# The sum of two weight blocks by an accumulating DMA, half-size weight tiles and alternating steps in a two-branch encoder block

## The chip, the cores and the metric

One core of one Trainium2 chip runs the kernel. The metric is the device time of one execution in microseconds; the median of three runs is compared.

## What is computed

The reference is one residual block of a streaming encoder on 256 tokens of width 4096, all in float32. Cut to what matters:

```python
h = rms_norm(x, pre_norm_gain)
proj = h @ w_in                      # 4096 x 24704, split into q, k, v, gate_a, qi, ki, wi,
                                     # z, xs, bm, cm, dt_raw, merge_logits (2 x 4096)
y_a = dsa_attention(q, k, v, qi, ki, wi) * silu(gate_a)      # [256, 2048]
y_b = ssd_mixer(xs, z, bm, cm, dt_raw, ...)                  # [256, 2048]
gates = sigmoid(merge_logits).reshape(b, s, 2, 4096)
merged = gates[0] * (y_a @ w_branch_attn) + gates[1] * (y_b @ w_branch_ssd)
out = merged @ w_out                                         # 4096 x 4096
x = x + rms_norm(out, post_norm_gain)
```

## The kernel before

Every matmul of the projections is computed as three: activation and weight are each split into a high part (float32r) and a low part, and `low x high + high x low + high x high` is accumulated in PSUM. The high part of a weight chunk (`wh`) is a ScalarE copy, the low part (`wl`) a VectorE subtraction. A matmul has 128 tokens as its stationary and 512 weight columns as its moving side.

*Plain stages.* `gemm` (L138) computes 512 output columns for both token tiles from eight chunks of 1 MB (`raw`, 128 x 4 x 512, pool `rawp` with three buffers, L54), loaded by SP. A chunk is split in two halves of 128x1024 (L168, L169). The index projection, the attention projections, the SSD projections and the first gate columns run so, up to about 1611 us, and the last two column blocks of the output projection at the end. In the first `gemm`, `prep_x` (L223) also loads the transposed input `xr` and issues the weight load itself; for chunk 0 it issues slices of both in turn. `make_rstd` (L244) loads the input rows once more in eight pieces `xn` for the row norms.

*Pair stages.* `pair_gemm` (L738) takes 512 columns of two blocks at a time, and two 128-row tiles of the contraction a step, so the weight chunk of a step is a 2x2 block matrix b11, b12, b21, b22 (`_quads`, L1072, lays the blocks out as b12, b11, b22, b21), and the activations of the two token tiles are a 2x2 block matrix too. A step of kind "S" multiplies them with seven products: the weights are b11, b21, b22 and four sums t1 = b11 - b12, t3 = b22 - b12, t2 = b22 + t1, t4 = b21 - t2; the activations are four blocks and four sums S1 to S4 that `make_ext` (L692) has formed. A step of kind "D" or "R" takes eight products. Sums over steps stay in PSUM, in banks 1 to 8, and `early` (L758) and `late` (L766) put the output blocks together from them: `early` after the last S step, `late` at the end of the group. `SX`, `SY` and `SM` (L34 to L36) say which of the 16 steps are S, for the gates, the branch projections and the output projection; `plain` ranges make some of them R.

The pair stages are: seven gate groups of 16 steps (`GATES`), eight branch groups of eight steps, three output groups of 16 steps. There are 90 S steps (21 matmuls each) and 134 others (24 each).

In an S step VectorE forms t1 and t3 in one operation `t13` (L792), and t2 (L795) and t4 (L797) in place in `raw`; four calls of `split` (L728; L731 on ScalarE, L732 on VectorE) make the high and low parts, in tiles of the pools `whp` and `wlp`, four buffers each. A step of eight products has two calls of `split`.

*Order.* Waits come from the tile framework. It lays out each engine's instructions when the kernel is built, and each engine runs its own in that order. Small work (rotary, attention, scan, epilogues, forms) is written as generators, and `step()` runs one piece of them after each half chunk or step. POOL's queue holds the stores of the gates to DRAM (`sscr`, L852), of the merged rows (`mscr`, L926) and the loads of activations for the forms (`fr`, L866 and L871). SP's queue holds the weight loads (L154, L786) and the loads of gates (L907).

## Time and profile before

| | |
|---|---|
| median of three runs | 2912.79 us (2911.95 to 2913.32) |
| the profiled execution | 2915.75 us, of it 2914.0 us of span from the first to the last instruction |
| TensorE, matmul rows | 2875.6 us busy, 99% |
| TensorE, weight-load rows | 2356.7 us, 81% |
| VectorE | 2039.2 us, 70% |
| ScalarE | 1499.5 us, 51% |
| GpSimd | 210.4 us, 7% |
| granted TensorE clock | 0.998 of full speed |
| DMA | 592 MB, 203 GB/s on average |

A busy share counts the time in which at least one row of the engine is open. Matmul rows overlap, since one begins while the one before still drains; so TensorE's share says little of its pace, and the distance between the starts of two matmuls says more.

### The profile page before, as it was taken

Reading aid. Unit: us, or ns where it says so; the run is one execution under the profiler, and the core shown is the slowest. Engines: PE = TensorE matmul, PEld = TensorE weight load, DVE = VectorE, ACT = ScalarE, POOL = GpSimd, SP = SyncE. Lnnn points to the kernel's source line nnn. Section 1 sums busy time; section 2 is a strip of 40 time slices with the busy share of each in tenths; the row PEclk is TensorE's granted clock in tenths of the full one; section 3 lists DMA queues with packets and bytes.
Section 4 is the critical chain, followed back from the end, with each engine's and each line's share of the span. In section 5 each row is a group of like instructions: output and inputs, shape, how many; then the busy total and the mean of one; then the engine's idle time right before and its main releaser. Section 6 shows DMA issues by size and latency. Waiting matters only on the chain. (4 is left out here: it accounts for less than half of the span.)

```text
span 2914.0 us, 33808 instructions
## 1 busy us (share of the span) xinstructions
PE 2875.6 (99%) x12990; PEld 2356.7 (81%) x12990; DVE 2039.2 (70%) x2490; ACT 1499.5 (51%) x1799; POOL 210.4 (7%) x209
## 2 busy tenths in 40 slices
PE   9999999999999999999999999999999999999997
PEld 7878888888888888888888888878887777788786
DVE  6677445454554646565657998989887888888975
ACT  7444443444434445454555555555565544555554
POOL 0100001000010012121211000000000000000001
PEclk9999999999999999999999999999999999999999
DMA  9545555555555555555555565555566556655664
GB/s 343 187 159 176 188 185 183 194 177 194 175 195 188 181 177 179 186 181 178 177 191 193 202 224 217 217 218 213 222 239 229 223 216 224 254 220 197 221 248 159
DMA packets 96098, 592.25 MB, mean 203 GB/s; under 512 B 11328, under 2 KB 12096, under 8 KB 30528
## 3 DMA queue, kind: packets, MB, share of 16 engines
q1 hardware_dynamic: 88992, 567.02, 54.2%
q0 software_dynamic: 6944, 23.07, 2.2%
q8 instruction: 102, 1.67, 0.2%
q14 instruction: 60, 0.49, 0.0%
HBM read 570.12 MB, written 19.92 MB: 202 GB/s over the span
## 5 line engine op out<-in xcount | busy, mean ns | idle before, releaser
L169 DVE TENSOR_TENSOR wl<-raw,wh 128x1024 fp32r<-128x1024 f32 x563 | 699.0, 1243 | 597.5 <-ACT wh L168 595.3
L168 ACT ACTIVATE wh<-raw 128x1024 fp32r<-128x1024 f32 x563 | 596.5, 1060 | 795.6 <-PE p L179 754.6
L177 PE MATMUL p<-wh,b 128*128 128x512 f32 x2304 | 911.1, 396 | 1.4 <-ACT wh L165 1.4
L178 PE MATMUL p<-wl,b 128*128 128x512 f32 x2304 | 898.7, 390 | 3.5 <-DVE wl L169 3.3
L179 PE MATMUL p<-wh,b 128*128 128x512 f32 x2304 | 898.4, 390 | 0.0
L756 PE MATMUL p<-wh,b 128*128 128x512 f32 x2300 | 757.2, 391 | 4.5 <-ACT wh L731 3.2
L731 ACT ACTIVATE wh<-raw 128x1024 fp32r<-128x1024 f32 (+1 forms) x538 | 510.5, 984 | 312.9 <-PE p L756 214.4
L732 DVE TENSOR_TENSOR wl<-raw,wh 128x1024 fp32r<-128x1024 f32 (+1 forms) x538 | 584.3, 1130 | 82.5 <-ACT wh L731 79.5
L756 PEld LDWEIGHTS p<-wh,b 128*128 128x128 f32 x2300 | 430.6, 188 | 101.3 <-ACT wh L731 11.2
L178 PEld LDWEIGHTS p<-wl,b 128*128 128x128 f32 x2304 | 433.3, 188 | 93.2 <-DVE wl L169 4.4
L177 PEld LDWEIGHTS p<-wh,b 128*128 128x128 f32 x2304 | 432.8, 188 | 92.3 <-ACT wh L165 3.0
L179 PEld LDWEIGHTS p<-wh,b 128*128 128x128 f32 x2304 | 432.6, 188 | 91.5
L756 PE MATMUL p<-wl,b 128*128 128x512 f32 x1150 | 448.5, 390 | 2.2 <-DVE wl L732 2.1
L756 PE MATMUL p<-wh,ext 128*128 128x512 f32 x1104 | 387.1, 391 | 4.8 <-ACT wh L731 4.8
L756 PEld LDWEIGHTS p<-wl,b 128*128 128x128 f32 x1150 | 215.9, 188 | 49.3 <-DVE wl L732 4.5
L756 PEld LDWEIGHTS p<-wh,ext 128*128 128x128 f32 x1104 | 207.2, 188 | 52.3 <-ACT wh L731 10.7
L756 PE MATMUL p<-wl,ext 128*128 128x512 f32 x552 | 217.2, 394 | 4.4 <-DVE wl L732 4.4
L731 ACT ACTIVATE wh<-t 128x1024 fp32r<-128x1024 f32 x90 | 95.5, 1061 | 146.0 <-PE p L756 120.8
L756 PEld LDWEIGHTS p<-wl,ext 128*128 128x128 f32 x552 | 103.6, 188 | 33.1 <-DVE wl L732 12.0
L792 DVE TENSOR_TENSOR t<-raw 128x1024 f32<-128x1024 f32 x90 | 109.9, 1221 | 28.7 <-DMA raw<-w_gate_d 14.7
L732 DVE TENSOR_TENSOR wl<-t,wh 128x1024 fp32r<-128x1024 f32 x90 | 109.9, 1222 | 16.5 <-ACT wh L731 15.7
L283 POOL TENSOR_TENSOR ro<-m,m 128x512 f32<-128x512 f32 (+1 forms) x26 | 43.0, 1666 | 413.9 <-DVE m L281 407.3
(224 smaller groups left out, 1415.1 us busy)
## 6 DMA issues: line engine op xcount, KB each, us to landing
raw<-w_attn_d SPq DMA_DIRECT2D x128, 1024.0 KB, 4.7
raw<-w_gate_d SPq DMA_DIRECT2D x128, 1024.0 KB, 4.8
raw<-w_ssd_d SPq DMA_DIRECT2D x96, 1024.0 KB, 4.7
raw<-w_br_d SPq DMA_DIRECT2D x64, 1024.0 KB, 4.8
raw<-w_out_d SPq DMA_DIRECT2D x64, 1024.0 KB, 4.8
raw<-w_qi_d SPq DMA_DIRECT2D x31, 1024.0 KB, 6.6
sg<-sscr SPq DMA_DIRECT2D x32, 256.0 KB, 3.4
sscr<-pc POOLq DMA_DIRECT2D x28, 256.0 KB, 2.9
```

Source lines behind the costliest of these rows:

```text
L168: A.activation(wh, rs, AF.Copy)
L169: V.tensor_sub(wl, rs, wh.bitcast(F32))
L177: T.matmul(ps[t], al[:, tk], wh[:, i, :], start=first, stop=False)
L178: T.matmul(ps[t], ah[:, tk], wl[:, i, :], start=False, stop=False)
L179: T.matmul(ps[t], ah[:, tk], wh[:, i, :], start=False, stop=last)
L283: G.tensor_add(ro, m1, m2)
L731: A.activation(h, src, AF.Copy)
L732: V.tensor_sub(l, src, fbit(h))
L756: T.matmul(ps[j], l, r, start=first and n == 0, stop=left[j] == 0 and n == 2)
L792: V.tensor_sub(t13, raw[:, 1:3, :], raw[:, 0:1, :].to_broadcast([P, 2, NW]))
```

## The change

It has five parts. (1) In an S step, b12's tile row gets the sum b12 + b11 by a DMA that POOL issues and that adds to what SP's load put there; the signs of b12 and b22's use are turned so that every combination is built on this sum. In eight-product steps the parts of b12 and b22 are split with a factor of -1, and the epilogue subtracts where it added. The four-row operation `t13` is gone; three one-row sums are left. (2) A weight chunk is two tiles of 512 KB, eight buffers of them, loaded one after the other. (3) The S steps of the gates and the output projection are the odd ones; those of the branches are 1, 4, 7, 9, 12, 15. (4) Products come in another order, and in a group's last S step products 1, 6, 7 come first, with `early` behind them. (5) To make room, `tab` and `mb` move to the attention pool, `xn` becomes sixteen pieces in the `yr` tiles, and the x slices of chunk 0 are all issued ahead of its weights.

```diff
+RBUFS = 8
...
-SX = (1, 3, 5, 6, 8, 10, 12, 14)
-SY = (1, 4, 6, 9, 12, 14)
-SM = (1, 3, 5, 6, 8, 10, 12, 14)
+SX = tuple(range(1, 16, 2))
+SY = (1, 4, 7, 9, 12, 15)
+SM = SX
...
-    rawp = root(tc.tile_pool(name="rawp", bufs=3))
+    rawp = root(tc.tile_pool(name="rawp", bufs=RBUFS))
...
+    def raw_tile():
+        return rawp.tile([P, HK, NW], F32, tag="raw", name="raw")
+
+    def load_half(raw, chunk, hf, each=False):
+        if each:
+            for i in range(HK):
+                nc.sync.dma_start(raw[:, i, :], chunk[:, hf * HK + i, :])
+        else:
+            nc.sync.dma_start(raw, chunk[:, hf * HK:(hf + 1) * HK, :])
...
-            raw = raws.get(c)
-            if raw is None:
-                raw = raws[c] = rawp.tile([P, KC, NW], F32, tag="raw", name="raw")
+            if half not in raws:
+                raws[half] = raw_tile()
                 if prep is not None:
-                    xr = prep(c, raw, chunks[c])
+                    if not hf:
+                        xr = prep_x(c)
+                    load_half(raws[half], chunks[c], hf, c == 0)
                 else:
-                    nc.sync.dma_start(raw, chunks[c])
+                    load_half(raws[half], chunks[c], hf)
             if half not in parts:
                 wh = whp.tile([P, HK, NW], F32R, tag="wh", name="wh")
                 wl = wlp.tile([P, HK, NW], F32R, tag="wl", name="wl")
                 parts[half] = wh, wl
                 if len(parts) > WBUFS:
                     del parts[next(iter(parts))]
-                rs = raw[:, hf * HK:(hf + 1) * HK, :]
+                rs = raws[half]
...
-    def prep_x(c, raw, chunk):
+    def prep_x(c):
         xr = sp.tile([P, KC, S], F32, tag="xr", name="xr")
         if c == 0:
             for i in range(KC):
                 nc.sync.dma_start(xr[:, i, :], xT[c][:, i * S:(i + 1) * S])
-                nc.sync.dma_start(raw[:, i, :], chunk[:, i, :])
         else:
             nc.sync.dma_start(xr.rearrange("p k t -> p (k t)"), xT[c])
-            nc.sync.dma_start(raw, chunk)
...
-            for h in range(4):
-                xn = sp.tile([P, D // 4], F32, tag="xn", name="xn")
-                nc.sync.dma_start(xn, x[t * P:(t + 1) * P, h * (D // 4):(h + 1) * (D // 4)])
+            for h in range(8):
+                xn = yr.tile([P, NW], F32, tag=f"yr{h}", name="xn")
+                nc.sync.dma_start(xn, x[t * P:(t + 1) * P, h * NW:(h + 1) * NW])
                 A.activation(xn, xn, AF.Square, accum_out=ss[:, t, h:h + 1])
-                yield
                 yield
...
-            V.scalar_tensor_tensor(f[:, 0, :], a21, -1.0, a22, ALU.mult, ALU.subtract)
+            V.tensor_sub(f[:, 0, :], a22, a21)
             V.tensor_sub(f[:, 2, :], a11, a21)
             V.scalar_tensor_tensor(f[:, 1, :], f[:, 0, :], -1.0, a11, ALU.mult, ALU.subtract)
-            V.tensor_sub(f[:, 3, :], a12, f[:, 1, :])
+            V.scalar_tensor_tensor(f[:, 3, :], a12, -1.0, f[:, 1, :], ALU.mult, ALU.subtract)
...
-    def split(src, n):
+    def split(src, n, sign=1):
         h = whp.tile([P, n, NW], F32R, tag="wh", name="wh")
         l = wlp.tile([P, n, NW], F32R, tag="wl", name="wl")
-        A.activation(h, src, AF.Copy)
-        V.tensor_sub(l, src, fbit(h))
+        A.activation(h, src, AF.Copy, scale=float(sign))
+        if sign < 0:
+            V.scalar_tensor_tensor(l, src, -1.0, fbit(h), ALU.mult, ALU.subtract)
+        else:
+            V.tensor_sub(l, src, fbit(h))
...
-                for o, j in zip(d, (2, 5, 4)):
-                    A.activation(o, ps[j], AF.Copy)
-                V.tensor_add(d[3], ps[8], d[1])
-                V.tensor_add(d[1], ps[3], d[1])
+                for o, j, sc in zip(d, (2, 5, 4), (1.0, -1.0, 1.0)):
+                    A.activation(o, ps[j], AF.Copy, scale=sc)
+                V.tensor_sub(d[3], d[1], ps[8])
+                V.tensor_sub(d[1], d[1], ps[3])
                 return
             c11, c12, c21, c22 = dest
             V.tensor_add(c12, ps[5], c12)
-            V.tensor_add(c22, ps[5], c21)
+            V.scalar_tensor_tensor(c22, ps[5], -1.0, c21, ALU.mult, ALU.subtract)
             V.tensor_add(c11, ps[2], c11)
             V.tensor_add(c21, ps[4], c21)
-            V.tensor_add(c12, ps[3], c12)
+            V.scalar_tensor_tensor(c12, ps[3], -1.0, c12, ALU.mult, ALU.subtract)
             if 8 in ps:
-                V.tensor_add(c22, ps[8], c22)
+                V.tensor_sub(c22, c22, ps[8])
...
+            ra, rb = raw_tile(), raw_tile()
+            load_half(ra, chunk(i), 0)
+            if kind == "S":
+                nc.gpsimd.dma_start(ra[:, 0, :], chunk(i)[:, 2, :], accum_op=ALU.add)
+            load_half(rb, chunk(i), 1)
             if n in hooks:
                 hooks[n]()
             assert kind_of[i] == what, (n, i, kind_of, len(aux))
             if kind == "S":
-                t13 = tp.tile([P, 2, NW], F32, tag="t13", name="t13")
-                V.tensor_sub(t13, raw[:, 1:3, :], raw[:, 0:1, :].to_broadcast([P, 2, NW]))
-                b11, b22 = split(raw[:, 1:3, :], 2)
-                b21, = split(raw[:, 3:4, :], 1)
-                V.tensor_add(raw[:, 2, :], raw[:, 2, :], t13[:, 0, :])
-                t1, t3 = split(t13, 2)
-                V.tensor_sub(raw[:, 3, :], raw[:, 3, :], raw[:, 2, :])
-                t2, t4 = split(raw[:, 2:4, :], 2)
-                for j, name, w in ((1, "A11", b11), (2, "A12", b21), (3, "S4", b22),
-                                   (5, "S1", t1), (7, "S3", t3), (6, "S2", t2), (4, "A22", t4)):
-                    product(j, i, name, w)
-                early()
+                b11, b21 = split(rb, 2)
+                t1, b22 = split(ra, 2)
+                V.tensor_add(ra[:, 1, :], ra[:, 0, :], ra[:, 1, :])
+                V.tensor_sub(rb[:, 0, :], ra[:, 1, :], rb[:, 0, :])
+                V.tensor_add(rb[:, 1, :], ra[:, 1, :], rb[:, 1, :])
+                t2, = split(ra[:, 1:2, :], 1)
+                t3, t4 = split(rb, 2)
+                now = {1: ("A11", b11), 2: ("A12", b21), 3: ("S4", b22), 4: ("A22", t4),
+                       5: ("S1", t1), 6: ("S2", t2), 7: ("S3", t3)}
+                for j in (1, 6, 7, 5, 3, 2, 4) if n == len(plan) - 1 else (1, 2, 5, 3, 6, 7, 4):
+                    product(j, i, *now[j])
+                    if j == 7:
+                        early()
             else:
                 w = {}
-                for k in (1, 2):
-                    w[k, 2], w[k, 1] = split(raw[:, 2 * k - 2:2 * k, :], 2)
-                todo = [(k, j) for k in (1, 2) for j in
-                        ((5, 2, 4, 3) if kind == "D" else (2, 4, 3, 8))]
-                if n == len(plan) - 1:
-                    todo.sort(key=lambda kj: (5, 2, 4, 3, 8).index(kj[1]))
+                w[1, 2], w[2, 2] = split(ra, 2, -1)
+                w[1, 1], w[2, 1] = split(rb, 2)
+                todo = [(k, j) for j in ((5, 3, 2, 4) if kind == "D" else (3, 8, 2, 4))
+                        for k in (1, 2)]
...
-            order = (0, 2, 4, 7, 1, 9, 3, 11, 5, 13, 6, 15, 8, 12, 10, 14)
-            plain = (8, 12, 10, 14)
+            order = (0, 2, 4, 6, 1, 8, 3, 10, 5, 12, 7, 14, 9, 11, 13, 15)
+            plain = (9, 11, 13, 15)
...
-    b = [v[:, 0][..., c2], v[:, 0][..., c1], v[:, 1][..., c2], v[:, 1][..., c1]]
+    b = [v[:, 0][..., c2], v[:, 1][..., c2], v[:, 0][..., c1], v[:, 1][..., c1]]
...
```

## Rows read from the trace of the kernel before

**Rows 1.** The page, busy time of an engine (share of the span) and its instructions.

```profile
PE 2875.6 (99%) x12990; PEld 2356.7 (81%) x12990; DVE 2039.2 (70%) x2490; ACT 1499.5 (51%) x1799; POOL 210.4 (7%) x209
```

**Rows 2.** Timeline of TensorE in a gate group: start us, us, what.

```profile
1814.20 0.39 PE L756 MATMUL p<-wh,b 128*128 128x512 f32 x1
...
1817.84 0.39 PE L756 MATMUL p<-wh,ext 128*128 128x512 f32 x1
```

**Rows 3.** Stretch, its us; busy us (count) of PE, PEld, DVE, ACT, POOL; clock, DMA, GB/s.

```profile
1610.90:2105.00 494.10, 490.34 (x2142) 399.24 (x2141) 445.91 (x479) 289.26 (x319) 13.04 (x24) 1.00 0.58 214
2105.00:2193.00 88.00, 86.17 (x375) 69.75 (x374) 78.40 (x111) 54.00 (x71) 8.77 (x16) 1.00 0.66 243
2193.00:2236.00 43.00, 41.26 (x180) 33.19 (x179) 29.33 (x39) 21.52 (x26) 3.27 (x6) 1.00 0.66 233
2236.00:2550.00 314.00, 305.54 (x1347) 247.10 (x1346) 273.74 (x329) 163.99 (x188) 9.83 (x18) 1.00 0.63 230
2550.00:2640.00 90.00, 90.00 (x405) 74.32 (x404) 72.11 (x86) 48.34 (x55) 0.00 (x0) 1.00 0.58 214
2640.00:2811.00 171.00, 168.85 (x733) 136.29 (x733) 154.58 (x169) 98.82 (x117) 0.00 (x0) 1.00 0.62 227
```

**Rows 4.** Timeline of TensorE, transposes in a branch group.

```profile
2295.39 0.60 PE L346 MATMUL p<-ct,pc 128*128 128x128 f32 x4
...
2296.09 0.40 PE L756 MATMUL p<-wh,ext 128*128 128x512 f32 x1
```

**Rows 5.** Timeline of TensorE, a pause in a gate group [idle before, releaser].

```profile
1811.74 0.73 PE L756 MATMUL p<-wh,b 128*128 128x512 f32 x2 [0.21 <-ACT wh L731]
```

**Rows 6.** Timelines of VectorE and of TensorE, later in a gate group.

```profile
2007.82 1.23 DVE L792 TENSOR_TENSOR t<-raw 128x1024 f32<-128x1024 f32 x1 [2.22 <-DMA raw<-w_gate_d]
...
2010.23 0.50 PE L756 MATMUL p<-wl,ext 128*128 128x512 f32 x1 [0.65 <-DVE wl L732]
```

**Rows 7.** Timeline of ScalarE at the start of a branch group.

```profile
2296.39 2.96 ACT L731 ACTIVATE wh<-raw 128x1024 fp32r<-128x1024 f32 x3 [2.53 <-DVE raw L797]
```

**Rows 8.** Timeline of VectorE around the same boundary.

```profile
2283.20 0.68 DVE L776 TENSOR_TENSOR pc<-p,pc 128x512 f32<-128x512 f32 x1
2283.80 0.68 DVE L777 TENSOR_TENSOR pc<-p,pc 128x512 f32<-128x512 f32 x1
...
2297.48 5.76 DVE L732 TENSOR_TENSOR wl<-raw,wh 128x1024 fp32r<-128x1024 f32 x5 [1.18 <-ACT wh L731]
```

**Rows 9.** Operations by line and shape: count, busy us, mean ns, idle before.

```profile
L701 DVE SCALAR_TENSOR_TENSOR frm<-fr 128x128 f32<-128x128 f32 x20 | 5.7, 286 | 6.5 <-DMA fr<-mscr 4.8 <-DMA fr<-yscr 1.7
L702 DVE TENSOR_TENSOR frm<-fr 128x128 f32<-128x128 f32 x20 | 5.7, 283 | 0.1
...
L1038 DVE SCALAR_TENSOR_TENSOR og<-p,oro,pgn 128x512 f32<-128x512 f32 x2 | 1.5, 737 | 0.0
```

**Rows 10.** DMA issues, median us to landing; last, those of L871.

```profile
raw<-w_gate_d SPq DMA_DIRECT2D x128, 1024.0 KB, 4.8
...
mscr<-mT POOLq DMA_DIRECT2D x6, 512.0 KB, 2.9
...
DMA to landing us min/median/max: 2.9/3.6/6.3
```

**Rows 11.** Timeline of POOL, two issues of loads for the forms.

```profile
2297.57 1.10 POOL L871 DMA_DIRECT2D fr<-mscr  x2 [2.88 <-issue]
```

**Rows 12.** Waits: engine, line, releaser, us in total, times, longest.

```profile
POOL sscr L852 <- ACT pc L851: 482.2, 8, 81.6
```

**Rows 13.** Timeline of VectorE in a seven-product step.

```profile
1800.77 0.69 DVE L797 TENSOR_TENSOR raw<-raw 128x512 f32<-128x512 f32 x1
1801.38 1.22 DVE L732 TENSOR_TENSOR wl<-t,wh 128x1024 fp32r<-128x1024 f32 x1
```

**Rows 14.** The start: stretch as in rows 3, and timeline of TensorE.

```profile
0.00:30.00 30.00, 26.06 (x96) 18.65 (x97) 21.25 (x42) 22.23 (x46) 0.20 (x4) 1.00 0.90 345
...
14.21 0.73 PE L177 MATMUL p<-wh,b 128*128 128x512 f32 x2 [1.42 <-ACT wh L165]
```

More of the change, by code (lines that the diff above doesn't have):

```diff
@@ L81, in fused_block @@
     rw = const.tile([P, 96], F32, name="rw")
-    tab = const.tile([P, 2, 384], F32, name="tab")
     rstd = const.tile([P, 2], F32, name="rstd")
@@ L92, in fused_block @@
     de0 = const.tile([P, 32], F32, name="de0")
-    mb = [const.tile([P, (t + 1) * P], F32, name=f"mb{t}") for t in range(2)]
     ident = ct[:, CT_ID:CT_ID + P]
@@ L218, in fused_block @@
         T.matmul(wb, warm[:, 0:P], warm, start=True, stop=True)
+    attp_cm = tc.tile_pool(name="attp", bufs=2)
+    attp = attp_cm.__enter__()
+    tab = attp.tile([P, 2, 384], F32, bufs=1, name="tab")
+    mb = [attp.tile([P, (t + 1) * P], F32, bufs=1, name=f"mb{t}") for t in range(2)]
     startp = tc.tile_pool(name="startp", bufs=2)
     sp = startp.__enter__()
-    def prep_x(c, raw, chunk):
+    def prep_x(c):
         xr = sp.tile([P, KC, S], F32, tag="xr", name="xr")
@@ L244, in make_rstd @@
     def make_rstd():
-        ss = sp.tile([P, 2, 4], F32, tag="ss", name="ss")
+        ss = sp.tile([P, 2, 8], F32, tag="ss", name="ss")
         for _ in range(12):
@@ L261, in make_rstd @@
         yield
-    attp_cm = tc.tile_pool(name="attp", bufs=2)
-    attp = attp_cm.__enter__()
     def rope(ps, t, heads, half, cofs, sofs):
@@ L488, in fused_block @@
     for j in range(2):
-        gemm([w_qi[j, c] for c in range(8)], KT, act, qi_rope(j), prep=None if j else prep_x)
+        gemm([w_qi[j, c] for c in range(8)], KT, act, qi_rope(j), prep=None if j else True)
     gemm_misc(evac_misc)
@@ L514, in to_ssd @@
         finish_older()
+        startp.__exit__(None, None, None)
         attp_cm.__exit__(None, None, None)
-        startp.__exit__(None, None, None)
         ssdp_cm, ssdp = open_pool("ssdp")
@@ L776, in late @@
             V.tensor_add(c12, ps[5], c12)
-            V.tensor_add(c22, ps[5], c21)
+            V.scalar_tensor_tensor(c22, ps[5], -1.0, c21, ALU.mult, ALU.subtract)
             V.tensor_add(c11, ps[2], c11)
             V.tensor_add(c21, ps[4], c21)
-            V.tensor_add(c12, ps[3], c12)
+            V.scalar_tensor_tensor(c12, ps[3], -1.0, c12, ALU.mult, ALU.subtract)
             if 8 in ps:
-                V.tensor_add(c22, ps[8], c22)
+                V.tensor_sub(c22, c22, ps[8])
         for n, (i, kind) in enumerate(plan):
-            raw = rawp.tile([P, KC, NW], F32, tag="raw", name="raw")
-            nc.sync.dma_start(raw, chunk(i))
+            ra, rb = raw_tile(), raw_tile()
[3 more added lines that the diff above has]
+            load_half(rb, chunk(i), 1)
             if n in hooks:
```

## The prediction

> **What bounds the kernel now.** I read the busy shares first. TensorE's row says 99% [rows 1], but a matmul row lasts 0.39 us while the next one starts 0.227 us after it: sixteen starts lie between the two rows of [rows 2], 3.64 us. So the distance between starts is the measure, and at that distance TensorE is the bound almost everywhere. The reader is to see from the code that the change leaves the number of matmuls alone. SX, SY and SM keep 8, 6 and 8 members, the plain ranges still strike out four, three, three and four of them, and so there are 90 seven-product steps of 21 matmuls and 134 eight-product steps of 24 before and after, 5106 in all. The change can only win back time in which TensorE does not start a matmul, or lose more of it.
>
> How much that is, I worked out from the stages of the pair steps [rows 3]: the window's length, less its matmuls at 0.227 us, less 0.47 us for each four transposes. The transposes' price is read from [rows 4]: from their start to the second matmul behind them it is 0.70 us, where one matmul alone would have put 0.23. Gate groups (1610.9 to 2105): 494.1 - 2142 x 0.227 = 7.9 us lost. Last gate group and its tail: 88 - 375 x 0.227 = 2.9. First branch group: 43 - 180 x 0.227 = 2.1. Rest of the branch groups, 48 transposes in twelve fours: 314 - 1299 x 0.227 - 5.6 = 13.5. First output group, 16 transposes: 90 - 389 x 0.227 - 1.9 = none. Other output groups: 171 - 733 x 0.227 = 4.6. Together **about 31 us, 1.1% of the time, is all that can be had** in the steps that are changed.
>
> Then I asked what ends the pauses. VectorE is busy 80 to 90% in all of those windows but the short one [rows 3], and it is what is late. Three patterns: (a) in a gate group the second of two adjacent seven-product steps (5 and 6 in SX) waits 0.38 us for a split ([rows 5] is one of seven, about 83 us apart); (b) VectorE stands 2.22 us in front of a weight chunk that has not landed, and then TensorE idles 0.65 us for the low half that VectorE should have made [rows 6]; (c) at the start of each branch group the seven-product step 1 waits for the split of t2 and t4, whose sums VectorE finished late, after the epilogue [rows 7].
>
> **The change part by part.**
> *VectorE.* Queued back to back, an operation of 128x512 costs 0.60 us and a split of 128x1024 costs 5.76 / 5 = 1.15 [rows 8]. A seven-product step now has t13 (1.15), two sums (1.20), three wide splits (3.45) and one narrow (0.60): 6.40. Afterwards three sums (1.80) and the same splits: 5.85. That is 0.55 us x 90 = 50 us of VectorE. Per pair of a seven- and an eight-product step VectorE goes from 8.70 to 8.15 us, against 45 x 0.227 = 10.2 on TensorE. VectorE is not the bound on average, so the 50 us are not the gain; what they do is shorten the lateness in (a) to (c).
> *Signs.* Turned signs make some subtractions three-operand ones. With an immediate those cost 286 ns beside 283 for the plain kind at the same shape [rows 9]: nothing. The other end is the form with a scalar per partition, 737 ns at 128x512 [rows 9] beside 0.68 us [rows 8]: 55 ns x about 160, 9 us of VectorE in eight-product steps, where it has 5.45 - 2.30 us free: off the path.
> *Alternation.* It removes (a): adjacent steps asked 6.40 us of VectorE in 4.77 us of TensorE. 7 x 0.38 in the gates and twice more in the output groups, about 3.5 us.
> *Half-size tiles.* Eight halves are four steps of weights instead of three, and a half comes free earlier. A chunk lands 4.8 us after issue, and a store of 512 KB in 2.9 [rows 10]. So (b) should go: of the 7.9 + 4.6 us lost in the gates and the output groups 9 are left without (a), and I take 5 of them. On SP, loads double in number and have nothing but waits around them: no cost.
> *The accumulating DMA.* No row of before shows one. The nearest is a 256 KB load issued by POOL, 0.55 us for the issue and 2.9 to 6.3 us to landing, median 3.6 [rows 10, 11]. It has to read its target too, so the top is twice the longest, 12.6; the bottom is 2.9; I take 4.5, near the median. It is put behind the landing of its own half: 2.9 to 4.8 + 0.55 + 4.5 = 8 to 10 us. Ahead of it stand four steps of buffers, 20.4 us, less the 6 us for which a step holds its tile: 14 us. So it is hidden with 4 us to spare; at the top end it is not (rival 3). What its issue does to VectorE: in [rows 11] two issues lie under the five splits of [rows 8] that run at their usual 1.15 us, so I take 0; the other end is not a gain, and 90 x 0.55 us of VectorE if every issue held it, which would undo the saving and leave (a) to (c) where they are, less the alternation.
> *New wait.* Queued behind the accumulate on POOL are gate stores and the loads of forms, and the accumulate stands behind them. Nobody waits soon for a store. But POOL waited 482 us in eight turns for the sigmoids [rows 12], so where a store precedes an accumulate the lead is gone. The order of rows shows that instructions are laid out by readiness and not by text (in the text the sum of L797 comes after the split of t13; in [rows 13] it runs ahead of it), so I expect most accumulates ahead of the stores and charge 2 us.
> *Order of products.* The last step of a group is now of seven products, with 6 and 7 right after 1. t3 and t4 use the tile that the step before frees at its end, so the low half of t3 is there 1.06 + 1.22 = 2.3 us into the step, and product 7 wants it at 1.6: at most 0.7 us in 14 groups, 10 us; none where other products are moved forward. I take 0.3 each, 4 us. In exchange the epilogue of a branch group moves towards the boundary by two sums, while step 1 needs 0.55 us less and no t13 first; I take 3 of the 13.5 us of (c) as won.
> *The forms.* The last gate group and the first branch group hold no seven-product steps in their later part; their 5 us of pauses also come from loads of forms. I take 1.5.
> *Start.* TensorE stands 1.42 us for the first split of chunk 1, whose load landed as one megabyte [rows 14]. A half would be there earlier by 512 KB at 345 GB/s = 1.5 us, less the extra issue: 1.0 us won. x tiles of chunk 0 go ahead of the weights, which delays the first matmuls by about 1 us; the later stall for chunk 1 hides that.
>
> Sum: 3.5 + 5 + 3 + 1.5 + 1 - 2 - 4 = **8 us won, with a little over for pauses under 0.13 us that I did not list: 9**. The profiled execution took 2915.75 us (span 2914.0), so 2906.7 there; it lies 2.96 above the median of the runs, so **2904 us**. Its own range, from none to all of the charged costs and from half to all of (c): 2898 to 2909.
>
> A rule against the half-size loads stands in the Trainium skill, "DMA: Bandwidth & Descriptors", Rules for kernel authors: for full bandwidth use 128 partitions and at least 1 MiB in one DMA. The rows here say that the rate matters only at the start, where the DMA engines are 90% busy; in the pair steps they are at 58 to 66%. By the rule the start would get slower: that is rival 4.
>
> **The rivals.**
> 1. *All pauses of (a) to (c) go*, VectorE now being ahead all the time. For it: the long pauses follow VectorE's waits for chunks. Against: (c) is an epilogue that stays. 31 - 7 (forms and boundaries at their least) + 1 = 25 us: 2888. Chance 0.12.
> 2. *Hidden anyway.* The pauses belong to the group boundary and to the in-order queues and come back elsewhere: what VectorE gets free turns into idle time, which it already has (10 to 20%). Only the start and the alternation gain, and the last steps take it back: 2911. Chance 0.17.
> 3. *Slower: accumulates late on POOL.* If they stand behind the stores of the group before, an accumulate is issued after the last sigmoid, lands some 5 us later, and the split that reads it is wanted 4 us earlier: 6 gate boundaries x 4 and 3 branch boundaries x 3 = 33 us, less the 9 won: 2937. It decides as soon as issue and landing take longer than the lead that is left. An accumulate of 12.6 us in every step would do the same: 3 us over the lead, once in every round of four steps, 45 rounds: far more. For it: POOL's long waits in order. Against: the readiness order above. Chance 0.16, mostly in a milder form, from 2919 up.
> 4. *Half-size loads hold up the start.* In the first 30 us the DMA engines are busy 90% at 345 GB/s [rows 14]; two lone halves take 2 x 2.9 = 5.8 us where a chunk takes 4.8, 21% more, of 30 us 6 us, and the gain of 9 shrinks to 3 with no gain at the start: 2911. Chance 0.05.
> Forecast: 0.50.
>
> **How the numbers follow.** 0.2% (5.8 us) is about what a measurement of this kernel can tell from no change: faster is under 2907.0, slower over 2918.6. Faster: 0.46 of the forecast's 0.50, and rival 1, 0.12: 0.58. Within: 0.04, rivals 2 and 4: 0.26. Slower: 0.16. The range leaves out the far half of rival 1 and all but the mildest of rival 3, about 0.19: 2893 to 2918.
>
> **What would show it.** Right: the pauses of (a) gone; no idle time of VectorE in front of weight loads; accumulates landing in 4 to 5 us, with the first split of their half not waiting for them; VectorE some 50 us less busy; group starts in the branch part still 1 to 2 us late. Wrong: idle time of ScalarE or VectorE ended by an accumulate (rival 3), new pauses before product 7 in last steps, VectorE's splits longer than 1.22 us while POOL issues, or gate groups still 83 us long (rival 2).

## The result and the profile after

| | before | after |
|---|---|---|
| median | 2912.71 us in the same job | **2935.22 us** (2932.24 to 2935.89) |
| ratio | 1 | **1.0075**, 95% interval 1.0058 to 1.0093 |
| the profiled execution, its span | 2915.75, 2914.0 us | 2932.24, 2929.7 us |

The change made the kernel 22 us slower; 9 us less were forecast, and the time lies outside the range (2893 to 2918). The profiled execution of after is the fastest of its kernel, and that of before is slower than its median, so the two profiles stand 16.5 us apart, and that is what can be divided up below.

The page of after, beside [rows 1, 10]: busy time by engine, then the DMA packets, the queue of DMAs that POOL issues, and three DMA issues (count, KB, median us to landing).

```profile
PE 2880.3 (98%) x12990; PEld 2355.7 (80%) x12990; DVE 2006.8 (68%) x2490; ACT 1505.4 (51%) x1815; POOL 290.6 (10%) x299
...
q0 software_dynamic: 19904, 46.67, 6.9%
...
raw<-w_gate_d SPq DMA_DIRECT2D x256, 512.0 KB, 5.0
...
raw<-w_gate_d POOLq DMA_DIRECT2D x52, 256.0 KB, 7.3
```

VectorE has 32.4 us less to do, less than the 50 that were meant. POOL is busy 80 us more, TensorE and ScalarE 5 to 6, and the DMA engines work more too. The stages, beside [rows 3]: stretch, its us, busy us (count) of PE, PEld, DVE, ACT, POOL, granted clock, DMA share, GB/s.

```profile
1611.00:2105.00 494.00, 489.79 (x2142) 399.72 (x2141) 427.67 (x474) 288.92 (x314) 53.35 (x69) 1.00 0.82 240
2105.00:2193.00 88.00, 85.95 (x374) 69.59 (x373) 78.53 (x118) 55.60 (x75) 12.06 (x20) 1.00 0.76 253
2285.00:2555.00 270.00, 254.70 (x1099) 198.52 (x1098) 222.98 (x281) 133.92 (x155) 22.22 (x32) 1.00 0.73 238
...
2816.00:2835.00 19.00, 14.95 (x59) 11.50 (x58) 15.59 (x20) 10.13 (x16) 0.00 (x0) 0.91 0.64 207
```

The gates hold the same 2142 matmuls in 494 us as before, so they neither won nor lost. In the branch groups TensorE has a row open for less of the time (254.70 of 270 us, where [rows 3] has 305.54 of 314). What the reader must see besides is the DMA share: 0.58 before, 0.82 now, for 214 and 240 GB/s.

**Where the time went.** A group's loss is the time from its first matmul to the next group's first one, less its matmuls at 0.2266 us (183 in the 41.48 us of a branch group of before that has no pause). The transposes among them are not taken off; they are the same in both kernels:

| us lost | before | after |
|---|---|---|
| gate groups 1 to 6, together | 9.2 | 9.9 |
| gate group 7 | 4.8 | 2.5 |
| eight branch groups, together | 21.4 | 36.0 |
| three output groups, together | 7.3 | 6.5 |

That is 12.3 us more. Behind the groups after is 5.2 us longer, up to the first pair step it is 1.7 us shorter, and 0.8 us lie outside the span: 16.5 together. Three places account for most of it.

*The group's start.* Timelines of TensorE and VectorE in after at a gate boundary: start us, us, what [idle before, releaser].

```profile
1937.30 1.22 DVE L744 TENSOR_TENSOR wl<-raw,wh 128x1024 fp32r<-128x1024 f32 x1 [1.33 <-ACT wh L740]
1938.44 0.68 DVE L775 TENSOR_TENSOR pc<-p,pc 128x512 f32<-128x512 f32 x1
1939.04 1.21 DVE L742 SCALAR_TENSOR_TENSOR wl<-raw,wh 128x1024 fp32r<-128x1024 f32 x1
1940.18 0.68 DVE L776 TENSOR_TENSOR pc<-p,pc 128x512 f32<-128x512 f32 x1
...
1940.73 0.39 PE L768 MATMUL p<-wh,b 128*128 128x512 f32 x1
...
1941.38 0.68 DVE L788 TENSOR_TENSOR pc<-p,pc 128x512 f32<-128x512 f32 x1
...
1941.86 1.35 PE L768 MATMUL p<-wh,b 128*128 128x512 f32 x3 [0.73 <-ACT wh L740]
1941.97 0.68 DVE L789 SCALAR_TENSOR_TENSOR pc<-p,pc 128x512 f32<-128x512 f32 x1
```

The group's last matmul starts at 1940.73. The next group's first products go into bank 5, and bank 5 is read by the sums L788 and L789, which need what `early` (L775, L776) makes from products 6 and 7. All of this stands in VectorE's order behind the split of t3 and t4 at 1937.30, and so L789 ends at 1942.65, 1.5 us after TensorE is through. TensorE's order has put two matmuls of later products ahead, which fill a part; the first of them itself waits for a ScalarE split (1941.86), and the first one into bank 5 starts only when L789 ends. Measured as the distance between two starts less 0.2266 us, the first start is 0.89 us late and the first one into bank 5 another 0.28: 1.17 us are lost. There are thirteen such starts, behind the groups that end on a seven-product step: 15.2 us. In the gates they take the place of the pauses of before [rows 5, 6], which are gone. A pause of 1.18 + 0.40 us at 2197.9 is not new, since before loses 1.35 us at 2198.60.

*The end of the pair steps.* The same views where the plain stage follows the last output group:

```profile
2823.82 0.61 PE L187 MATMUL p<-wh,b 128*128 128x512 f32 x2
...
2824.49 2.81 DVE L994 TENSOR_TENSOR og<-og,pgc 128x512 f32<-128x512 f32 x4
2827.22 2.35 DVE L179 TENSOR_TENSOR wl<-raw,wh 128x1024 fp32r<-128x1024 f32 x2
...
2828.49 0.71 PE L188 MATMUL p<-wl,b 128*128 128x512 f32 x1 [4.05 <-DVE wl L179]
2829.00 0.63 PE L189 MATMUL p<-wh,b 128*128 128x512 f32 x1
2829.43 0.63 PE L188 MATMUL p<-wl,b 128*128 128x512 f32 x1
```

The epilogue and four products with `pgc` stand ahead of the split that TensorE waits for: 4.2 us, where before had 0.7. Behind it eight starts are 0.427 us apart (the first 0.51) in place of 0.227, the lower of the clock's two levels (1.2 GHz; the granted clock of 2816 to 2835 us is 0.91): 1.7 us more.

*The old pause (c).* In after a branch group still loses at its first seven-product step:

```profile
2341.26 0.50 PE L768 MATMUL p<-wh,ext 128*128 128x512 f32 x1 [0.27 <-ACT wh L740]
2342.45 0.50 PE L768 MATMUL p<-wl,ext 128*128 128x512 f32 x1 [0.68 <-DVE wl L744]
2343.97 0.50 PE L768 MATMUL p<-wh,b 128*128 128x512 f32 x1 [0.21 <-ACT wh L740]
```

0.44 + 0.96 + 0.38 = 1.8 us, and in the same place before 0.35 + 0.73 + 0.38 = 1.5.

### The profile page after: what moved, and what is told of

The parts are those of the page before. It is cut to its first block, busy times and chain, and to the rows that moved or that the text cites. A ratio compares the mean times of both kernels' runs of the same rounds, so it can differ in the third digit from the quotient of the medians.

```text
span 2929.7 us, 35727 instructions
## 1 busy us (share of the span) xinstructions
PE 2880.3 (98%) x12990; PEld 2355.7 (80%) x12990; DVE 2006.8 (68%) x2490; ACT 1505.4 (51%) x1815; POOL 290.6 (10%) x299
## 5 line engine op out<-in xcount | busy, mean ns | idle before, releaser
L740 ACT ACTIVATE wh<-raw 128x1024 fp32r<-128x1024 f32 (+1 forms) x628 | 609.9, 995 | 475.5 <-PE p L768 223.2
L744 DVE TENSOR_TENSOR wl<-raw,wh 128x1024 fp32r<-128x1024 f32 (+1 forms) x494 | 543.2, 1123 | 144.7 <-ACT wh L740 136.9
L768 PE MATMUL p<-wh,ext 128*128 128x512 f32 x1104 | 374.6, 392 | 1.9 <-DVE pc L792 1.0
L742 DVE SCALAR_TENSOR_TENSOR wl<-raw,wh 128x1024 fp32r<-128x1024 f32 x134 | 163.6, 1221 | 21.6 <-ACT wh L740 14.7
L800 POOL DMA_DIRECT2D raw<-w_gate_d x52 | 45.6, 878 | 472.6 <-DMA raw<-w_gate_d 182.3
L809 DVE TENSOR_TENSOR raw<-raw 128x512 f32<-128x512 f32 x90 | 62.2, 691 | 2.8
```

Source lines behind the costliest of these rows:

```text
L740: A.activation(h, src, AF.Copy, scale=float(sign))
L742: V.scalar_tensor_tensor(l, src, -1.0, fbit(h), ALU.mult, ALU.subtract)
L744: V.tensor_sub(l, src, fbit(h))
L768: T.matmul(ps[j], l, r, start=first and n == 0, stop=left[j] == 0 and n == 2)
L800: nc.gpsimd.dma_start(ra[:, 0, :], chunk(i)[:, 2, :], accum_op=ALU.add)
L809: V.tensor_sub(rb[:, 0, :], ra[:, 1, :], rb[:, 0, :])
```

## The experiments

Each ratio is to the kernel before in the same job, with its 95% interval.

**The lists and the accumulate, one at a time.** First, after with the lists of before.

```diff
-SX = tuple(range(1, 16, 2))
-SY = (1, 4, 7, 9, 12, 15)
+SX = (1, 3, 5, 6, 8, 10, 12, 14)
+SY = (1, 4, 6, 9, 12, 14)
```

(SM, `order` and `plain` go back with them.)

> The changed kernel with the step lists of before (groups end on an eight-product step again; accumulating DMA, half tiles, turned signs and product orders stay). Theory (the epilogue of a group that ends on a seven-product step is not covered: 14 pauses of 1.17 us at group starts, and 4.2 us plus a lower clock for some 2 us at the first plain step behind the last group): those go, the two adjacent seven-product steps come back with at most 9 x 0.38 us: 2911 to 2917 us, and group starts without a pause of 1.17 us. Rival (the accumulating DMA and the crowded DMA engines, share 0.82 in the gates instead of 0.58, make the loss): stays at 2930 or more.

Measured 2916.61 us, 1.0006 (0.9997 to 1.0016), as the theory has it: some 20 of the 22 us come with the lists, and all else in the change adds up to nothing. Most gate groups now lose 1.06 us each, in one place, where two seven-product steps are adjacent; this is the second half of it:

```profile
1812.52 0.50 PE L768 MATMUL p<-wh,b 128*128 128x512 f32 x1 [0.21 <-ACT wh L740]
```

Then the kernel before with nothing but the new lists (the same five lines the other way round).

> The kernel before with nothing but the new step lists (strict alternation, groups ending on a seven-product step; no accumulating DMA, full tiles). Theory (group ends): pauses at 14 group starts of 1 us or more and a longer one behind the last group, less the 9 x 0.38 us of the adjacent steps: 2925 to 2940 us. Rival (accumulating DMA): 2908 to 2913, the alternation being a small gain.

Measured 2956.58 us, 1.0144 (1.0128 to 1.0160): 42 us, far above what was expected. TensorE at the same boundary:

```profile
1950.31 0.50 PE L756 MATMUL p<-wl,b 128*128 128x512 f32 x1 [1.72 <-DVE wl L732]
...
1951.51 0.80 PE L756 MATMUL p<-wh,b 128*128 128x512 f32 x1 [0.46 <-DVE pc L778]
1952.10 0.63 PE L756 MATMUL p<-wl,b 128*128 128x512 f32 x1
1952.53 1.05 PE L756 MATMUL p<-wh,b 128*128 128x512 f32 x2
```

Without the early products 6 and 7 and with the longer VectorE work a start costs 1.94 + 0.63 us, and behind some of these starts, this one among them, matmuls at the lower clock follow. So the new lists cost 42 us alone and 20 with the rest of the change; which part of the change makes the difference, the next two runs tell.

Next, the sum by VectorE in place of the accumulate, with the new lists and with the old.

```diff
-            if kind == "S":
-                nc.gpsimd.dma_start(ra[:, 0, :], chunk(i)[:, 2, :], accum_op=ALU.add)
...
+                V.tensor_add(ra[:, 0, :], ra[:, 0, :], rb[:, 0, :])
```

> The changed kernel with the sum of b12 and b11 made by VectorE instead of the accumulating DMA (one operation of 128x512 more in each of 90 steps, 0.60 us each, nothing on POOL). Theory (group ends): all 14 pauses stay, VectorE is 54 us busier, 2935 to 2942 us. Rival (accumulating DMA): falls to 2905 to 2915, and DMA share in the gates falls back to about 0.6.

> Both of the two together: step lists of before, and the sum by VectorE; what is left of the change is half-size tiles with one step more of lead, the signs, the product orders. Theory (group ends): within 5 us of the run with the old step lists, 2910 to 2920. Rival (accumulating DMA): within 5 us of the run with the sum on VectorE. If both count and add up, this is the fastest of the four.

Measured 2965.46 us, 1.0180 (1.0162 to 1.0199), and 2922.81 us, 1.0028 (1.0018 to 1.0038), both above what was expected. The accumulate is worth 30 us with the new lists and 6 with the old; that it makes the loss is out. Half-size tiles, signs and orders without it are 8 us worse than before.

Between these two runs the new lists cost 43 us, as much as on the kernel before. So the new orders alone leave the lists' loss where it was; it is the accumulate, which takes a sum off VectorE in each seven-product step, that halves it. In e2_dve_sum a group's start costs what it costs in after (second line), and the rest stands in front of low halves in seven-product steps along the groups (first line):

```profile
1949.85 0.50 PE L768 MATMUL p<-wl,ext 128*128 128x512 f32 x1 [0.68 <-DVE wl L744]
...
1954.97 1.34 PE L768 MATMUL p<-wh,b 128*128 128x512 f32 x3 [0.71 <-ACT wh L740]
```

**What at a group's end.** After without the sums that read banks 5 and 3 (products 3 and 5 don't reach the output, so its time is that of a kernel with less to do):

```diff
-            V.tensor_add(c12, ps[5], c12)
-            V.scalar_tensor_tensor(c22, ps[5], -1.0, c21, ALU.mult, ALU.subtract)
+            A.activation(c22, ps[4], AF.Copy)
...
-            V.scalar_tensor_tensor(c12, ps[3], -1.0, c12, ALU.mult, ALU.subtract)
```

> The kernel after, with its own lists, but the three sums of the epilogue that read banks 5 and 3 are left out (products 3 and 5 don't reach the output; c22 is a ScalarE copy instead). Theory (a group's start waits for banks that these sums on VectorE still read): the 14 pauses of 1.17 us go, and the tail loses 1.8 us less: 2914 to 2920. Rival (the start waits for weight tiles that the last step's products 3, 2, 4 free too late, the part ended by ScalarE's split): 0.73 of each 1.17 stays, 2927 to 2932.

Measured 2918.56 us, 1.0013 (1.0003 to 1.0023), some 17 us under after, as the theory has it. Across the same boundary TensorE does not pause, the part that a ScalarE split ended included:

```profile
1941.33 0.39 PE L768 MATMUL p<-wl,b 128*128 128x512 f32 x1
1941.56 0.62 PE L768 MATMUL p<-wh,b 128*128 128x512 f32 x2
1942.01 0.39 PE L768 MATMUL p<-wl,b 128*128 128x512 f32 x1
```

TensorE's order is laid out anew with fewer sums. ScalarE's split comes no earlier against the group's end, which is the last matmul at 1940.73 in after and at 1941.56 here; first after, then e8_odd_no_late:

```profile
1939.80 2.95 ACT L740 ACTIVATE wh<-raw 128x1024 fp32r<-128x1024 f32 x3 [1.10 <-PE p L768]
```
```profile
1940.62 2.01 ACT L740 ACTIVATE wh<-raw 128x1024 fp32r<-128x1024 f32 x2 [1.11 <-PE p L768]
```

So the wait for ScalarE in after is that of the matmuls that were moved ahead; where the bank is free in time TensorE goes on without it.

Then strict alternation with the eight-product step last:

```diff
-SX = tuple(range(1, 16, 2))
-SY = (1, 4, 7, 9, 12, 15)
+SX = tuple(range(0, 16, 2))
+SY = (1, 4, 6, 9, 12, 14)
```

(`order` and `plain` go with them.)

> The kernel after, but the seven-product steps are the even ones (gates, output projection) and 1, 4, 6, 9, 12, 14 (branches): strict alternation stays in the gates and the output, no group ends on a seven-product step. Theory (the place of the last seven-product step makes the loss, alternation itself is good): the old lists gave 2916.6 with 1.06 us lost in each gate group at adjacent seven-product steps; without those, 7 gate and 2 output groups x 0.7 = 6 us less, 2908 to 2913. Rival 1 (alternation brings nothing): 2915 to 2918. Rival 2 (strict alternation itself makes the loss, wherever a group ends): 2928 or more.

Measured 2914.85 us, 1.0000 (0.9990 to 1.0009). This expectation's rival 2 is out, and its rival 1 comes nearest. Of the theory the place of the last seven-product step holds, 20 us under after; that alternation is good in itself is not met: gate groups lose 1.8 us each, more than the 1.06 with adjacent steps, because the pause moved to the step the group now begins with:

```profile
1698.24 0.50 PE L768 MATMUL p<-wl,ext 128*128 128x512 f32 x1 [0.69 <-DVE wl L744]
...
1699.76 0.50 PE L768 MATMUL p<-wh,b 128*128 128x512 f32 x1 [0.21 <-ACT wh L740]
```

With eight seven-product steps in sixteen, either two are adjacent (1.06 us), or the group begins with one (1.8), or ends with one (1.7). The list of before was the cheapest of the three.

**What the accumulating transfer costs.** The kernel of e5_even_sets without the accumulate; the sum is left out of the computation.

```diff
-            if kind == "S":
-                nc.gpsimd.dma_start(ra[:, 0, :], chunk(i)[:, 2, :], accum_op=ALU.add)
```

> The kernel of e5_even_sets without the accumulating DMA and without anything in its place: the sum b12 + b11 is left out of the computation, so this prices the transfer itself. Theory A (the accumulates crowd the DMA engines, share 0.65 to 0.80, and make form and weight loads late at the last gate group and in the branch groups): 4 to 8 us less than e5_even_sets, with the long pauses at 2138 to 2147 and 2312 gone. Theory B (the transfers are hidden; those pauses come from the order of work): within 2 us of e5_even_sets, pauses stay.

Measured 2915.40 us, 0.9998 (0.9989 to 1.0007): as long as with them. The transfers cost nothing there, theory B, though they take 0.15 of the DMA engines (e1_old_sets against e3_old_sets_dve). The pauses of the last gate group stay as well: it loses 6.0 us without accumulates and 5.2 with them (e5_even_sets). The gates (columns as above) in e3_old_sets_dve, e1_old_sets, e10_old_full and e7_even_no_sum, one each:

```profile
1611.00:2105.00 494.00, 489.75 (x2137) 398.96 (x2136) 452.50 (x525) 289.36 (x316) 12.20 (x23) 1.00 0.65 214
```
```profile
1611.00:2105.00 494.00, 491.09 (x2149) 401.28 (x2148) 431.40 (x481) 292.59 (x317) 54.33 (x71) 1.00 0.80 240
```
```profile
1611.00:2105.00 494.00, 489.96 (x2138) 399.62 (x2137) 429.23 (x477) 290.64 (x316) 53.48 (x69) 1.00 0.74 238
```
```profile
1611.00:2105.00 494.00, 487.71 (x2129) 397.83 (x2128) 425.67 (x473) 290.51 (x314) 11.92 (x22) 1.00 0.65 216
```

Then the lead and the size of a load, both on e1_old_sets: six half-size buffers, and four whole ones.

```diff
-RBUFS = 8
+RBUFS = 6
```

```diff
-            ra, rb = raw_tile(), raw_tile()
-            load_half(ra, chunk(i), 0)
+            raw = raw_tile()
+            nc.sync.dma_start(raw, chunk(i))
+            ra, rb = raw[:, 0:HK, :], raw[:, HK:KC, :]
...
-            load_half(rb, chunk(i), 1)
```

(with RBUFS 4, tiles of 1 MB, and one load in `gemm` too)

> The kernel of e1_old_sets (after, with the lists of before) with six half-size buffers in place of eight, so three steps of weights in flight as before the change. Theory A (more weight loads in flight make the form loads land late, 7.4 us at 2302.8 where they took 3 to 4, and VectorE stands in front of them in its order): the last gate group loses 5 us or less in place of 7.9, the branch group after 2285 5 or less in place of 9.2, and the time is 5 to 8 us under e1_old_sets' 2916.6: 2909 to 2912. Theory B (half-size transfers make them late, however many): within 2 us of e1_old_sets. Theory C (the lead of four steps is needed by the accumulates): slower than e1_old_sets, 2920 or more, with ScalarE or VectorE waiting for accumulates in the gates.

> The kernel of e1_old_sets with weight chunks in one tile of 1 MB and one load again, four of them, so the same memory and the same lead in steps as eight halves; the accumulate waits for the whole load. Theory B (half-size transfers take more of the DMA engines, share 0.58 to 0.65 at the same bytes, and make the form loads late): DMA share of the gates down by 0.05 to 0.08, 4 to 8 us under e1_old_sets' 2916.6. Theory A (the number of loads in flight counts, not their size): within 2 us of it, with the same losses in the last gate group and the branch group after 2285.

Measured 2964.05 us, 1.0158 (1.0126 to 1.0190), and 2912.67 us, 0.9998 (0.9987 to 1.0009). Of six buffers theory C is right: some 45 us for a quarter of the lead. ScalarE's waits for weights in the gates (us in total, times, longest), first with six, then with eight buffers:

```profile
ACT wh L740 <- DMA raw<-w_gate_d: 53.7, 24, 7.2
```
```profile
ACT wh L740 <- DMA raw<-w_gate_d: 3.2, 2, 2.6
```

Whole tiles gain 2 to 4 us against e1_old_sets (by the ratios and by the medians; the intervals overlap), with the DMA share down from 0.80 to 0.74 at nearly the same rate. But in its profile, of an execution of 2920.6 us, the last gate group still loses 10.3 and the branch group at 2288 8.7 us; so theory B holds for the share and not for the form loads.

**The forms.** In the kernels with old lists those two groups lose the most. VectorE and POOL in e10_old_full:

```profile
2299.07 0.56 POOL L942 DMA_DIRECT2D mscr<-mT  x1 [4.11 <-ACT mT L359]
2303.05 1.11 POOL L887 DMA_DIRECT2D fr<-mscr  x2 [3.42 <-DMA mscr<-mT]
2311.81 0.29 DVE L712 TENSOR_TENSOR frm<-fr 128x128 f32<-128x128 f32 x1 [6.16 <-DMA fr<-mscr]
```

The layout has put the first forms of the output projection 200 us ahead of their use, in the middle of a branch group. Before, the same load [rows 11] was issued at 2297.57 and landed before VectorE reached it. Here it is 5.5 us later and its two loads are 7 and 8 us on their way, and VectorE stands 6.16 us in front of work that nobody needs. Two one-column copies that depend on a later load hold it back:

```diff
+                    for _ in range(2):
+                        d = tp.tile([P, 2, S], F32, tag="fr", bufs=2, name="fr")
+                        A.activation(d[:, 0, 0:1], sig[0, 0][:, 0:1], AF.Copy)
```

> The kernel of e10_old_full, with two one-column ScalarE copies into the two fr buffers in the branch group that begins near 2469, so the first loads of the output projection's forms, which the layout put into the branch group at 2288, stay behind them. Theory (VectorE stands 4.9 us in its order in front of a form that nobody needs for 200 us, because its load, issued behind a slow store, lands 7 us late): the branch group at 2288 loses 4 to 5 us in place of 8.7, and the time is 3 to 5 us under e10_old_full's 2912.7. Rival (the group's start is late through the epilogue of the group before, and the wait for the form fills time that would be lost anyway): the pauses near 2316 stay, within 1.5 us of e10_old_full.

Measured 2912.20 us, 0.9998 (0.9987 to 1.0008). The group loses 4.1 us in place of 8.7, as the theory has it, and the median is within the rival's 1.5 us of e10_old_full: part of the gain shows up as loss elsewhere (the branch group near 2461 loses 7.1 in place of 5.4 us), and executions of both kernels scatter over some 12 us. For the time it is inconclusive.

In the last gate group another one remains. POOL and ScalarE in e11_full_hold:

```profile
2126.21 0.91 POOL L803 DMA_DIRECT2D raw<-w_gate_d  x1 [1.74 <-DVE b L727]
2126.77 0.91 POOL L882 DMA_DIRECT2D fr<-yscr  x1
...
2135.89 0.63 ACT L726 ACTIVATE b<-fr 128x512 fp32r<-128x512 f32 x1 [6.74 <-DMA fr<-yscr]
```

The form load is issued behind two accumulates; ScalarE, whose next splits stand behind the form, waits 6.74 us. SP issues the form loads instead:

```diff
-        nc.gpsimd.dma_start(a.rearrange("p k t -> p (k t)"), yscr[i])
+        nc.sync.dma_start(a.rearrange("p k t -> p (k t)"), yscr[i])
```

(and the same for `mscr`)

> The kernel of e11_full_hold, with the loads of forms issued by SP in place of POOL. Theory (in the last gate group a form load stands behind an accumulate that waits for its half's load on POOL, and ScalarE then waits 5.3 to 8.3 us for the form): that wait goes under 1 us, the last gate group loses 5 us or less in place of 7.9 to 10.3, 3 to 5 us under e11_full_hold. Rival (on SP the form load stands behind weight loads that wait for buffers, and is as late): within 2 us of e11_full_hold, or slower.

Measured **2905.57 us, 0.9971 (0.9962 to 0.9981)**, 6.6 us under e11_full_hold. The group loses 4.1 us in place of 8.2. The longest wait for a form there is 2.19 us, not the under 1 us expected:

```profile
2142.41 0.63 ACT L726 ACTIVATE b<-fr 128x512 fp32r<-128x512 f32 x1 [2.19 <-DMA fr<-yscr]
```

Is that the change's gain, or that of the two edits? The two diffs above, on the kernel before and alone:

> The kernel before, with the two edits that made e12_full_hold_sp 9 us faster than before and nothing of the change: the output forms' first loads are held back, and SP issues the form loads. Theory (these edits mend what the accumulates and the extra loads did to the form loads; the kernel before has no 5 us waits for forms, its form loads land in 3 to 6 us): within 3 us of before. Rival (the win of e12_full_hold_sp is these edits alone, and the change gives nothing): 2905 to 2909, as e12_full_hold_sp.

Measured 2908.45 us, 0.9980 (0.9971 to 0.9989): 5.7 of the 9 us are theirs, more than the theory allowed and inside the rival's range; the last gate group of before loses 0.7 in place of 4.8 us, as large a gain as in e12_full_hold_sp, and without an accumulate on POOL. What is left to the change is 2.9 us, within the two intervals. And e12_full_hold_sp with VectorE's sum (the diff of e2_dve_sum):

> The kernel of e12_full_hold_sp with the sum b12 + b11 made by VectorE in place of the accumulating DMA. Theory (with the form loads out of POOL's queue and the old lists, VectorE's 0.60 us in each of 90 steps still counts where two seven-product steps are adjacent and at the branch groups' starts): 5 to 8 us slower than e12_full_hold_sp, 2911 to 2914. Rival (hidden): within 2 us of it.

Measured 2910.94 us, 0.9990 (0.9981 to 1.0000), at the edge of the theory: the accumulate is worth 5 us there (the two intervals just touch), and without it the rest of the change gives nothing over before with the same edits (2.5 us slower, overlapping intervals).

**The start.** x and weight slices of chunk 0 in turn again, on e5_even_sets and on e12_full_hold_sp:

```diff
+                        nc.sync.dma_start(xr[:, i, :], xT[0][:, i * S:(i + 1) * S])
                         nc.sync.dma_start(raw[:, i, :], chunks[c][:, i, :])
```

> The kernel of e5_even_sets, with the x slices and the weight slices of chunk 0 issued in turn, as before the change. Theory (loading all x slices first makes the first split of weights late and costs a long pause of TensorE of about 2.3 us and matmuls at a lower clock behind it): 3 to 4 us less than e5_even_sets, first pauses as before. Rival (the prediction's own: the later wait for chunk 1 hides it): within 1 us of e5_even_sets, with a longer pause at chunk 1.

> The kernel of e12_full_hold_sp with the x slices and the weight slices of chunk 0 issued in turn, as before the change. The pair e5_even_sets and e6_even_start showed 0.3 us for this with half-size tiles. With one tile of 1 MB the first split of chunk 1 waits for the whole megabyte, so at most what before lost there comes back: within 2 us of e12_full_hold_sp; if the low clock behind the first pause counts in full, 3 us less.

Measured 2914.53 us, 1.0000 (0.9990 to 1.0009), so nothing with half-size tiles, as the prediction said. With whole tiles **2903.67 us, 0.9958 (0.9944 to 0.9973)**, 3.8 us under e12_full_hold_sp by the ratios, whose intervals overlap, and 1.9 by the medians. This is the fastest kernel of the case, 10 to 12 us under before and 5 under before with the two edits: old lists, four whole tiles, the accumulate, and form loads out of POOL's queue.

## Why the prediction was wrong

**The step that failed** is *Order of products*. It asked only whether t3 and t4 come in time for the last step's product 7, charged 4 us, and booked the epilogue's move to the boundary as a gain for (c). It did not ask which banks the epilogue still reads when the next group wants them. By the prediction's own numbers an eight-product step leaves VectorE 5.45 - 2.30 = 3.15 us free for the epilogue, while a seven-product step asks 5.85 us of it in 4.77. The epilogue is seven sums, 0.60 us apart in [rows 8]. In the order that the trace of after shows, five of them and one split (1.15) stand between the split of t3 and t4 and the last read of bank 5: 4.15 us, where TensorE has at most the fifteen matmuls from product 7 on, 3.4 us. So at least 0.75 us in each of 14 groups could have been worked out from costs that were there. Measured: 1.17 us at each of thirteen starts, 15.2 in all, and 5.2 at the end of the pair steps, against 4 charged. e1, e4 and e8 show it; without the accumulate the same lists cost twice as much (e2 against e3).

The other terms, as the prediction has them:
- *VectorE, 50 us.* 32.4 us measured on the page; why not 50 was not pursued. That they shorten lateness holds (e2, e3).
- *Signs, nothing.* Right: the three-operand split takes 1221 ns (L742), the plain one of before 1222 (wl<-t).
- *Alternation, 3.5 us won.* Pause (a) did go, but a list without adjacent steps pays more at one end of the group (e5).
- *Half-size tiles, 5 us won.* Pause (b) is gone. But e3 is 8 us slower than before, and whole tiles with the same lead are 2 to 4 us better (e10). The rule that the prediction weighed, at least 1 MiB in one DMA (the Trainium skill, "DMA: Bandwidth & Descriptors", Rules for kernel authors), was set aside because the share was 0.58 to 0.66. By that rule the DMA engines are worse used in the pair steps too, and the trace agrees: 0.58 in before and 0.65 in e3_old_sets_dve for the same 214 GB/s.
- *The accumulate.* Landing was 7.0 us in the median (3.5 to 8.6), inside the bounds and far from the 4.5 I took. An issue holds POOL for 0.87 us, not 0.55. Still it is hidden (e7, with the even lists), by the lead of four steps and no more (e9): the working of the lead was right.
- *New wait, 2 us.* What was queued behind the accumulate was named, but priced at the stores. Moving the form loads out of POOL's queue won 6.6 us between e11 and e12. That the accumulate is what makes them dear is not shown: e7 without accumulates is no faster, and before, which has none, won 5.7 us by that move and the held-back loads (e13).
- *(c), 3 us won.* None; 1.8 us where 1.5 were.
- *Forms, 1.5.* The last gate group of after won 2.3 us.
- *Start, 1.0 won.* The first pair step begins 1.7 us earlier, though it shares that with all plain stages.

Rival 3 had the sign and nearly the time (2937), by another mechanism: in after no accumulate is late behind a store. Accumulates that come too late do occur with six buffers (e9), there through the shorter lead. Rival 2 had its own sign, gate groups still 83 us long, because what was won there came back at the group boundary; its time, 2911, leaves out what the branch groups and the end of the pair steps lost. Rival 4 is out, rival 1 too.

**Open.** Why half-size tiles, signs and orders together cost 8 us in e3 was settled only in part (2 to 4 us by e10); signs alone and the product order alone were not run. And in e12's profile one gate group loses 6.6 us in place of 1.1, since an accumulate issued at 1711.37 lands 8.4 us later; which executions have this was not pursued.

## What to carry to other kernels

When a list of alternating steps is changed, look first at what the last step of a group leaves uncovered: which PSUM banks its sums still read, how much of that engine's own work stands ahead of them, and which product the next group begins with. Look for in-order engines that wait for small loads: moving those loads to another queue and holding some back won 5.7 us on the kernel before, with nothing of the change. Price an edit that helps the changed kernel on the old one too, before its gain is booked to the change. A lead in buffers is worth a measurement of its own: a quarter less cost some 45 us here.

## What the runs showed of the hardware

An accumulating DMA takes more of the DMA engines for its bytes than a plain load. The two queues of after between 1611 and 2105 us (packets, MB, share of 16 engines):

```profile
q1 hardware_dynamic: 27448, 99.46, 63.9%
q0 software_dynamic: 8667, 18.53, 18.0%
```

That is 0.64% of the engines per MB for the loads and 0.97 for POOL's queue, of whose 69 issues 47 are accumulates. The same queue in e5_even_sets and, without the accumulates, in e7_even_no_sum:

```profile
q0 software_dynamic: 8688, 18.62, 17.8%
```
```profile
q0 software_dynamic: 1894, 6.19, 3.4%
```

The difference is 14.4% for 12.43 MB, so an accumulate takes 1.16% per MB, 1.8 times a load's. The share rose from 0.58 to 0.65 when the same bytes came in halves, and to 0.80 when 12% more bytes came by accumulation; the form loads of the last gate group took 2.9 to 5.7 us in before (median 3.5), 3.1 to 6.3 (4.7) in e7_even_no_sum with half-size tiles and no accumulates, and 2.9 to 8.7 (5.0) in e1_old_sets with both.

A pause can be followed by several matmuls at the lower clock: starts are 0.427 us apart behind the 4.2 us at 2828.49 in after, and 0.43 behind the 1.94 + 0.63 us at 1950.31 and 1951.51 in e4_before_odd, whose mean granted clock is 0.994 where before has 0.998. Behind the same pause at 1865.58 in e4_before_odd the starts go on 0.23 us apart.
